# Convolution, sixteen panels' low parts and decay masks: from GpSimd to VectorE in a gated delta rule

## The chip, the cores and the metric

One core of a Trainium2 chip runs the whole model. The metric is the device time of one execution in microseconds; the kernel before took 2576.89 us as the median of three runs (2573.45 to 2579.9). The engines are called PE (TensorE), DVE (VectorE), ACT (ScalarE), POOL (GpSimd) and SP (SyncE, which issues most DMAs).

## What is computed

A two-layer encoder on 1024 tokens of width 1024 in float32: chunked attention, a squared-ReLU MLP, a gated delta rule, a second MLP, with an RMS norm ahead of each. The change is in the delta rule, of which this matters:

```python
qkv = silu(causal_conv(h @ w_in))          # 4 taps: y = sum_j xp[:, j:j+S] * w[j]
q, k, v = split(qkv)                       # 8 heads of 128; q and k are normalised
decay = exp(where(incl, gc[i] - gc[j], -inf))
L = where(strict, (k * beta) @ k.T * decay, 0)      # per chunk of 64
u, w = triangular_solve(I + L, [beta * v, beta * k * exp(gc)])
for chunk:                                 # scan over 16 chunks
    v_new = u - w @ state
    o = (q * exp(gc)) @ state + (q @ k.T * decay) @ v_new
    state = state * g_last + (k * exp(g_last - gc)).T @ v_new
```

The mask of the decay is added before the exponential: 0 where a pair of tokens counts, a large negative number elsewhere.

## The kernel before

**Products.** Float32 products are made of three float32r matmuls: a weight panel of 128 output columns is split into a high part (ACT rounds it, `whi`) and a low part (what is left, `wlo = wraw - whi`, a subtraction of two SBUF tiles), and PE adds high by high, high by low and low by high. A panel has two parts of 128x512. A dense job of the delta rule (one head of k, q, v or z) is two halves of 512 tokens, each 24 matmuls into one of two `acc` banks. The order of jobs is: eight heads of k, then q and v of heads 0 to 2, then z, q, v in turn, and last two panels of the output projection (`dn_ahead`, L1758; the panel's steps are `weights`, L1775, with `low`, L1010).

**Evacuation.** `dn_evac` (L2071) empties a bank. For q, k and v, DVE multiplies the bank with the norm's factor into `xp`, which frees the bank for the half after next; then come the convolution's four taps. Before, ACT makes two of them (`cy`, `cz`), DVE adds one more to each with a scalar_tensor_tensor, and POOL adds the two sums. For k of heads 4 to 7 (`POOLED`, L38) POOL adds twice, ACT makes three taps and DVE one. ACT's silu writes the head.

**Decays.** `dn_loads` (L2012) brings a head's row of cumulated decays into a tile (`row` for even heads, `vT` for odd ones) once the head two before it has its `U`, as the tile is used again. `dn_decays` (L2023) adds the mask in two parts of 128x512, ACT takes exponentials (`row<-row,gcols`), SP stores pieces. `dn_blocks` (L2155) multiplies k by k on PE and DVE multiplies the result with the decays into `U`, of which SP stores the diagonal blocks (`ud`, `u12`), four and two DMAs a head.

**Solves, scans.** `dn_solves` (L2185) waits for the `U` of four heads, loads `fu`, and runs 31 steps of substitution on DVE, a product `ft` and a reduction `fz` each, the last on 128x961. There are two such solves. Behind a solve come the inverses, the preparation of keys, values and queries and, head by head, two at a time, the scans: 16 chunks of PE (`s<-st,WQ`), DVE (`vn`), PE (`s<-vn,kd`), DVE (`st`).

**Order.** One loop (`dn_run`, L1809) emits the dense matmuls and after each lets waiting tasks take a step; a clock with a price for each instruction says which tasks are ready. The engines' programs are fixed by that: each engine takes its instructions in the order in which they were emitted. A change of the engine of an instruction changes the clock and thereby the order of all that follows in the delta rule. The clock has no price for DMAs but fixed sleeps (3.2 us for the row of a head).

Of the kernel before, what the change touches and what calls it, by code (L numbers as in the profile page):

```python
# [10 lines left out]
AF = mybir.ActivationFunctionType  # L11
ALU = mybir.AluOpType
# [8 lines left out]
HB = 512  # L21
# [13 lines left out]
ATT = (3, 2, 0.5, 1, 1, 0.7, 0.6)  # L35
RINGS = {"pt": 2, "po": 2, "sp": 1, "pr": 6, "bias": 3, "thi": 4, "tlo": 3, "oh": 1, "ot": 2}
ENGINES = {"dn_solves": ("vector",), "dn_decays": ("scalar",)}
POOLED = (4, 5, 6, 7)  # L38


def wide(col, p, n):
# [166 lines left out]
class Trunk:  # L208
# [1549 lines left out]
    def dn_ahead(self):  # L1758

        H = 8  # L1760
        self.jobs = jobs = [("k", n) for n in range(H)] + [(c, n) for n in range(3) for c in "qv"]
        for n in range(3, H):
            jobs += [("z", n - 3), ("q", n), ("v", n)]
        jobs += [("z", n) for n in range(5, H)]
        jobs += [("o", m) for m in range(2)]
        raw, panel = {}, {}

        def fetch(n):
            if n < len(jobs):
                c, h = jobs[n]  # L1770
                raw[n] = self.wp.tile([P, KT, P], F32, name=self.nm("wraw"), tag="wraw")
                self.nc.sync.dma_start(
                    raw[n], self.a["w_od"][h] if c == "o" else self.a["w_in"][8 * "qkvz".index(c) + h])

        def weights(n):  # L1775
            hi = self.wp.tile([P, KT, P], F32R, name=self.nm("whi"), tag="whi")
            lo = self.wp.tile([P, KT, P], F32R, name=self.nm("wlo"), tag="wlo")
            panel[n] = hi, lo
            for s in (slice(0, 4), slice(4, 8)):
                self.high(hi[:, s], raw[n][:, s])  # L1780
                yield
                self.low(lo[:, s], raw[n][:, s], hi[:, s], True)
                yield
                yield
            fetch(n + 2)

        def first():

            nc = self.nc
            ab = self.wp.tile([P, KT, P], F32, name=self.nm("wraw"), tag="wraw")  # L1790
            nc.sync.dma_start(ab[:, :, 0:16], self.a["w_ab"])
            for _ in range(8):
                yield
            fetch(0)
            yield
            yield
            self.wab = w = self.wp.tile([P, KT, P], F32R, name=self.nm("whi"), tag="whi")
            nc.gpsimd.memset(w[:, :, 16:32].bitcast(F32), 0.0)
            self.high(w[:, :, 0:16], ab[:, :, 0:16])
            yield  # L1800
            self.low(w[:, :, 32:48], ab[:, :, 0:16], w[:, :, 0:16], True)
            yield
            fetch(1)
            yield from weights(0)

        self.panel, self.weights = panel, weights
        return first()
# [215 lines left out]
    def dn_decays(self, odd):  # L2023

        nc = self.nc
        yield from self.until("rows")
        for h in range(odd, 8, 2):
            yield from self.until("load", h)
            if h < 2:
                yield from self.until("cols")  # L2030
            d = self.heads.pop(("load", h))
            v = d.rearrange("p (q t) -> p q t", t=P)
            for q in range(2):
                u = v[:, 4 * q : 4 * q + 4]
                nc.gpsimd.tensor_tensor(
                    u, u, self.mask.rearrange("p (o t) -> p o t", o=1).broadcast_to([P, 4, P]), ALU.add)
                yield
            for p in range(8):
                nc.scalar.activation(v[:, p], v[:, p], AF.Exp, bias=self.cols[:, 0, h, p : p + 1])
            yield  # L2040
            for e in range(2):
                r = slice(64 * e, 64 * e + 64)
                nc.sync.dma_start(self.decay[h, r], v[r, :, r])
            yield
            self.heads["de", h] = d
            self.mark("de", h)
            yield
# [23 lines left out]
    def dn_evac(self, c, h, half, ps):  # L2071

        nc = self.nc
        s = slice(half * HB, (half + 1) * HB)
        if c == "z":
            if half == 0:
                if h == 1:
                    yield from self.until("solve", 1)
                if h >= 2:
                    yield from self.until("out", h - 2)  # L2080
                self.heads[c, h] = self.dn_out_of(c, h)
            while (c, h) not in self.heads:
                yield
            t = self.heads[c, h][:, s]
            nc.vector.tensor_tensor(t, ps, self.R[:, s], ALU.mult)
            self.give("acc", ps)
            yield
            nc.scalar.activation(t, t, AF.Silu)
        else:
            w = self.convw[:, 8 * "qkv".index(c) + h]  # L2090
            xp = yield from self.take("xp")
            if half == 0:
                nc.vector.memset(xp[:, 0:3], 0.0)
            else:
                nc.vector.tensor_copy(xp[:, 0:3], self.edge[:, HB : HB + 3])
            self.edge = xp
            nc.vector.tensor_tensor(xp[:, 3 : 3 + HB], ps, self.R[:, s], ALU.mult)
            self.give("acc", ps)
            yield
            yt = yield from self.take("cy")  # L2100
            zt = yield from self.take("cz")
            y, z = yt[:, :HB], zt[:, :HB]
            nc.scalar.activation(y, xp[:, 3 : 3 + HB], AF.Copy, scale=w[:, 3:4])
            nc.scalar.activation(z, xp[:, 1 : 1 + HB], AF.Copy, scale=w[:, 1:2])
            yield
            if c == "k" and h in POOLED:
                nc.gpsimd.tensor_tensor(z, y, z, ALU.add)
                yield
                nc.scalar.activation(y, xp[:, 0:HB], AF.Copy, scale=w[:, 0:1])
                nc.vector.scalar_tensor_tensor(z, xp[:, 2 : 2 + HB], w[:, 2:3], z, ALU.mult, ALU.add)  # L2110
            else:
                nc.vector.scalar_tensor_tensor(y, xp[:, 2 : 2 + HB], w[:, 2:3], y, ALU.mult, ALU.add)
                nc.vector.scalar_tensor_tensor(z, xp[:, 0:HB], w[:, 0:1], z, ALU.mult, ALU.add)
            self.give("xp", xp)
            yield
            nc.gpsimd.tensor_tensor(y, y, z, ALU.add)
            self.give("cz", zt)
            yield
            if half == 0:
                for need in self.dn_room(c, h):  # L2120
                    yield from self.until(*need)
                self.heads[c, h] = self.dn_out_of(c, h)
            while (c, h) not in self.heads:
                yield
            nc.scalar.activation(self.heads[c, h][:, s], y, AF.Silu)
            self.give("cy", yt)
            self.silu_at = self.clock.at["scalar"]
        if half == 1:
            self.mark(c, h)
# [532 lines left out]
```

## Time and profile before

The profiled execution took 2579.18 us, its span is 2577.4 us, 2.3 us of the time above the median of the runs. The delta rule with its surroundings runs from about 1210 to 1850 us of the span.

| what | us or share |
|---|---|
| median of the runs (three) | 2576.89 us |
| profiled execution, span | 2579.18 us, 2577.4 us |
| busy share of the span, PE, DVE, ACT, POOL | 96%, 74%, 47%, 50% |
| additions of POOL for the convolution, whole span | 48 of `cy`, 68.9 us, and 8 of `cz`, 11.0 us |
| masks on POOL | 8 on `row`, 10.4 us, and 8 on `vT`, 10.7 us |
| low parts on POOL from 1210 to 1850 us | 66, 89.8 us |

A busy share is an average over stages, and matmuls overlap: PE counts as busy when one is under way. The page's lists of waits name the instruction that came last; the order of an engine's program decides what stands behind it.

### The profile page before, as it was taken

How to read it: one execution, taken by the hardware profiler on the slowest of the kernel's cores; microseconds unless marked ns; L12 is line 12 of the kernel's file. 1: busy time of each engine (PE TensorE's matmuls, PEld its weight loads, DVE VectorE, ACT ScalarE, POOL GpSimd, SP SyncE). 2: the span in 40 equal slices, each digit the busy share in tenths (PEclk: the TensorE clock that was granted, in tenths of full speed). 3: DMA queues.
4: the chain of work that ended last, by engine and by line, in shares of the span. 5: the costliest groups of instructions: out<-in, count | busy, mean ns of one | idle time of the engine just before them, and what ended most of it. 6: DMA issues, size and time to landing. Idle time of an engine off the chain costs nothing.

```text
span 2577.4 us, 36731 instructions
## 1 busy us (share of the span) xinstructions
PE 2472.7 (96%) x12638; PEld 2063.6 (80%) x12638; DVE 1914.8 (74%) x3297; ACT 1210.1 (47%) x2269; POOL 1298.2 (50%) x1090
## 2 busy tenths in 40 slices
PE   8999999999999999998888999999899999999997
PEld 6888888787888788886677788888787888787885
DVE  6665556677878788877578976666678787778877
ACT  6666567535555433334673333333335555433333
POOL 2444355515677476556464333332314766466656
PEclk9999999999999999999998999999999999999998
DMA  4222224424555976743343121122323555967742
GB/s 160 68 65 73 71 84 129 140 82 167 210 203 215 358 233 227 249 147 111 116 142 106 55 82 60 59 85 94 119 98 143 208 209 200 345 235 253 249 160 82
DMA packets 193082, 392.43 MB, mean 152 GB/s; under 512 B 54960, under 2 KB 61552, under 8 KB 192896
## 3 DMA queue, kind: packets, MB, share of 16 engines
q1 hardware_dynamic: 176048, 355.46, 41.0%
q10 hardware_dynamic: 16848, 34.63, 3.4%
q8 instruction: 100, 1.64, 0.3%
q14 instruction: 86, 0.70, 0.1%
HBM read 254.06 MB, written 127.57 MB: 148 GB/s over the span
## 4 chain that ended last, share of the span: by engine, by line
PE 61%; DVE 11%; DMA 3%; issue 3%; ACT 1%; POOL 1%; SPq 0%; ACTq 0%; DVEq 0%; POOLq 0%
PE y L1008 24%; PE z L1008 11%; PE acc L163 9%; PE acc L1008 6%; PE tp L163 4%; PE s L163 3%; DVE ft L163 2%; PE acc L279 1%; PE acc L277 1%; PE acc L278 1%; DVE x L1512 1%; DMA wraw<-in_w_up_dram 1%; DVE wlo L1014 1%; DVE fz L163 1%; DVE xs L393 1%
## 5 line engine op out<-in xcount | busy, mean ns | idle before, releaser
L163 PE MATMUL acc<-xs,whi 128*128 128x512 f32 x1808 | 633.9, 414 | 10.4 <-DVE xp L163 9.8
L163 PEld LDWEIGHTS acc<-xs,whi 128*128 128x128 f32 x1808 | 334.8, 192 | 60.0 <-DVE xp L163 6.1
L163 PE MATMUL acc<-xs,wlo 128*128 128x512 f32 x896 | 369.6, 413 | 2.1 <-POOL wlo L163 2.1
L1008 PE MATMUL y<-xs,whi 128*128 128x512 f32 x1008 | 312.0, 390 | 5.2 <-DVE x L1512 1.8
L163 POOL TENSOR_TENSOR wlo<-wraw,whi 128x512 fp32r<-128x512 f32 x126 | 167.7, 1331 | 246.3 <-ACT whi L163 197.3
L1023 POOL TENSOR_TENSOR s<-wraw 128x256 f32<-128x256 f32 (+1 forms) x93 | 89.4, 962 | 352.9 <-DVE a L1014 171.9
L1014 DVE TENSOR_TENSOR wlo<-wraw,whi 128x512 fp32r<-128x512 f32 (+1 forms) x182 | 209.4, 1151 | 27.3 <-ACT whi L1017 27.3
L1008 PEld LDWEIGHTS y<-xs,whi 128*128 128x128 f32 x1008 | 189.2, 188 | 47.1 <-DVE x L1512 2.6
L1017 ACT ACTIVATE whi<-wraw 128x512 fp32r<-128x512 f32 (+2 forms) x191 | 146.5, 767 | 123.8 <-PE y L1008 86.6
L1008 PE MATMUL y<-xs,wlo 128*128 128x512 f32 x504 | 197.0, 391 | 6.2 <-DVE wlo L1014 6.2
L1008 PE MATMUL y<-xs,a 128*128 128x512 f32 x732 | 189.0, 394 | 10.0 <-DVE x L1512 9.8
L1017 ACT ACTIVATE a<-s 128x256 fp32r<-128x256 f32 x122 | 63.8, 524 | 281.5 <-PE y L1008 141.7
L163 PEld LDWEIGHTS acc<-xs,wlo 128*128 128x128 f32 x896 | 172.6, 193 | 27.0 <-POOL wlo L163 2.5
L1512 DVE TENSOR_TENSOR x<-y,x 128x512 f32<-128x512 f32 x240 | 165.0, 688 | 36.8 <-PE y L1008 28.6
L1008 PEld LDWEIGHTS y<-xs,a 128*128 128x128 f32 x732 | 136.6, 189 | 44.5 <-DVE x L1512 14.2
L1008 PE MATMUL acc<-xs,whi 128*128 128x512 f32 x528 | 162.9, 390 | 0.0
L1008 PE MATMUL y<-xs,ahi 128*128 128x512 f32 x512 | 159.2, 392 | 0.7 <-ACT nt L1201 0.4
L1090 DVE TENSOR_TENSOR c<-c 128x512 fp32r<-128x512 f32 x112 | 132.8, 1203 | 28.5 <-POOL c L1020 28.5
L163 POOL TENSOR_SCALAR pr<-pr,rs 128x640 f32<-128x640 f32 (+4 forms) x128 | 88.1, 692 | 129.4 <-DVE rs L163 96.7
L1008 PE MATMUL z<-xs,whi 128*128 128x512 f32 x480 | 148.8, 391 | 0.0
L163 POOL TENSOR_TENSOR cy<-cy,cz 128x512 f32<-128x512 f32 x48 | 68.9, 1435 | 146.7 <-DVE cz L163 124.3
L163 DVE CUSTOM_DVE_ANT_0 pr<-sp,bias 128x640 f32<-128x640 f32 (+4 forms) x128 | 83.8, 655 | 63.8 <-PE sp L163 62.8
(340 smaller groups left out, 6295.2 us busy)
## 6 DMA issues: line engine op xcount, KB each, us to landing
xs<-gt SPq DMA_DIRECT2D x256, 256.0 KB, 4.9
gt<-c SPq DMA_DIRECT2D x112, 512.0 KB, 3.0
wraw<-in_w_up_dram SPq DMA_DIRECT2D x64, 512.0 KB, 3.5
wraw<-in_w_down_dram SPq DMA_DIRECT2D x64, 512.0 KB, 4.4
r<-gr SPq DMA_DIRECT2D x88, 256.0 KB, 3.4
wraw<-in_w_in_dram SPq DMA_DIRECT2D x32, 512.0 KB, 3.4
gr<-ssum ACTq DMA_DIRECT2D x62, 256.0 KB, 3.2
wraw<-in_w_qkv_dram SPq DMA_DIRECT2D x30, 512.0 KB, 3.4
```

The costliest lines, as they stand in the source:

```text
L163: return call(*args, **more)
L277: nc.tensor.matmul(ps, hi[:, k], xh, start=(k == 0), stop=False)
L278: nc.tensor.matmul(ps, hi[:, k], xl, start=False, stop=False)
L279: nc.tensor.matmul(ps, lo[:, k], xh, start=False, stop=(k == KT - 1))
L393: self.nc.vector.scalar_tensor_tensor(lo, x, w, hi.bitcast(F32), ALU.mult, ALU.subtract)
L1008: nc.tensor.matmul(ps, w[:, k], x, start=bool(first and f), stop=bool(last and e), skip_group_check=True)
L1014: self.nc.vector.tensor_tensor(lo, src, hi.bitcast(F32), ALU.subtract)
L1017: self.nc.scalar.activation(hi, src, AF.Copy)
L1023: self.nc.gpsimd.tensor_tensor(out, x, y, ALU.add)
L1090: nc.vector.tensor_tensor(t[z][:, HB:].bitcast(F32R), t[z][:, HB:], t[z][:, :HB], ALU.subtract)
L1512: nc.vector.tensor_tensor(x, ps, x, ALU.add)
```

## The change

DVE makes what POOL made in three places: the taps of the convolution are one product on ACT and three scalar_tensor_tensor in a chain on DVE (no `cz`, no addition on POOL); the low parts of panels 0 to 15 are subtracted on DVE, later ones stay on POOL; the masks are added on DVE. All else moves only because the clock orders it anew.

```diff
--- before.py
+++ after.py
@@ -35,7 +35,6 @@
 ATT = (3, 2, 0.5, 1, 1, 0.7, 0.6)
 RINGS = {"pt": 2, "po": 2, "sp": 1, "pr": 6, "bias": 3, "thi": 4, "tlo": 3, "oh": 1, "ot": 2}
 ENGINES = {"dn_solves": ("vector",), "dn_decays": ("scalar",)}
-POOLED = (4, 5, 6, 7)
 
 
 def wide(col, p, n):
@@ -1779,7 +1778,7 @@
             for s in (slice(0, 4), slice(4, 8)):
                 self.high(hi[:, s], raw[n][:, s])
                 yield
-                self.low(lo[:, s], raw[n][:, s], hi[:, s], True)
+                self.low(lo[:, s], raw[n][:, s], hi[:, s], n >= 16)
                 yield
                 yield
             fetch(n + 2)
@@ -2032,7 +2031,7 @@
             v = d.rearrange("p (q t) -> p q t", t=P)
             for q in range(2):
                 u = v[:, 4 * q : 4 * q + 4]
-                nc.gpsimd.tensor_tensor(
+                nc.vector.tensor_tensor(
                     u, u, self.mask.rearrange("p (o t) -> p o t", o=1).broadcast_to([P, 4, P]), ALU.add)
                 yield
             for p in range(8):
@@ -2098,23 +2097,12 @@
             self.give("acc", ps)
             yield
             yt = yield from self.take("cy")
-            zt = yield from self.take("cz")
-            y, z = yt[:, :HB], zt[:, :HB]
+            y = yt[:, :HB]
             nc.scalar.activation(y, xp[:, 3 : 3 + HB], AF.Copy, scale=w[:, 3:4])
-            nc.scalar.activation(z, xp[:, 1 : 1 + HB], AF.Copy, scale=w[:, 1:2])
-            yield
-            if c == "k" and h in POOLED:
-                nc.gpsimd.tensor_tensor(z, y, z, ALU.add)
-                yield
-                nc.scalar.activation(y, xp[:, 0:HB], AF.Copy, scale=w[:, 0:1])
-                nc.vector.scalar_tensor_tensor(z, xp[:, 2 : 2 + HB], w[:, 2:3], z, ALU.mult, ALU.add)
-            else:
-                nc.vector.scalar_tensor_tensor(y, xp[:, 2 : 2 + HB], w[:, 2:3], y, ALU.mult, ALU.add)
-                nc.vector.scalar_tensor_tensor(z, xp[:, 0:HB], w[:, 0:1], z, ALU.mult, ALU.add)
+            yield
+            for n in (2, 1, 0):
+                nc.vector.scalar_tensor_tensor(y, xp[:, n : n + HB], w[:, n : n + 1], y, ALU.mult, ALU.add)
             self.give("xp", xp)
-            yield
-            nc.gpsimd.tensor_tensor(y, y, z, ALU.add)
-            self.give("cz", zt)
             yield
             if half == 0:
                 for need in self.dn_room(c, h):
```

Where the masks go. DVE before, from the evacuation `xp` of the seventh half (the first of k of head 3) on; `acc` are PE's banks, `U` the products with decays, `cy` and `cz` the taps:

```order
L163 TENSOR_TENSOR xp_12746<-acc_12675,R_12294 128x512
L163 TENSOR_TENSOR U_12730<-tp_12751,vT_12562 128x512
L163 SCALAR_TENSOR_TENSOR cy_12757<-xp_12746,convw,cy_12757 128x512
L163 SCALAR_TENSOR_TENSOR cz_12758<-xp_12746,convw,cz_12758 128x512
L163 COPY xp_12820<-xp_12746 128x3
L163 TENSOR_TENSOR xp_12820<-acc_12744,R_12294 128x512
L163 TENSOR_TENSOR U_12832<-tp_12833,row_12727 128x512
L163 SCALAR_TENSOR_TENSOR cy_12839<-xp_12820,convw,cy_12839 128x512
L163 SCALAR_TENSOR_TENSOR cz_12840<-xp_12820,convw,cz_12840 128x512
L163 MEMSET xp_12877 128x3
L163 TENSOR_TENSOR xp_12877<-acc_12806,R_12294 128x512
L163 TENSOR_TENSOR U_12832<-tp_12851,row_12727 128x512
```

The masks of these heads stood on POOL, here with what followed them:

```order
L163 TENSOR_TENSOR row_12727<-row_12727,mask 128x512 x2
L163 TENSOR_TENSOR cy_12757<-cy_12757,cz_12758 128x512
L163 TENSOR_TENSOR vT_12777<-vT_12777,mask 128x512 x2
L163 TENSOR_TENSOR wlo_12824<-wraw_12673,whi_12823 128x512
L163 TENSOR_TENSOR cy_12839<-cy_12839,cz_12840 128x512
L163 TENSOR_TENSOR wlo_12824<-wraw_12673,whi_12823 128x512
```

DVE after, from the evacuation of the same half on:

```order
L162 TENSOR_TENSOR xp_12736<-acc_12664,R_12294 128x512
L162 TENSOR_TENSOR row_12708<-row_12708,mask 128x512
L162 TENSOR_TENSOR U_12711<-tp_12739,vT_12569 128x512
L162 SCALAR_TENSOR_TENSOR cy_12745<-xp_12736,convw,cy_12745 128x512 x3
L162 TENSOR_TENSOR row_12708<-row_12708,mask 128x512
L162 COPY xp_12800<-xp_12736 128x3
L162 TENSOR_TENSOR xp_12800<-acc_12734,R_12294 128x512
L162 TENSOR_TENSOR vT_12769<-vT_12769,mask 128x512 x2
L162 SCALAR_TENSOR_TENSOR cy_12811<-xp_12800,convw,cy_12811 128x512 x3
L162 TENSOR_TENSOR wlo_12804<-wraw_12659,whi_12803 128x512
L162 MEMSET xp_12850 128x3
L162 TENSOR_TENSOR xp_12850<-acc_12793,R_12294 128x512
```

The masks of heads 2 (`row`) and 3 (`vT`) now stand between the evacuations, and each convolution is three instructions.

Where the scan of the last head goes. PE before, about the middle of the scan of head 7 (`s` are the banks of the scan, `acc` those of dense products):

```order
L163 MATMUL s_3785_17927<-st_17920,WQ_17613 128x128
L163 MATMUL acc_17844<-xs_11825,whi_17570 128x512
L163 MATMUL acc_17844<-xs_11825,wlo_17571 128x512
L163 MATMUL acc_17935<-xs_17868,whi_17765 128x512 x2
L163 MATMUL s_3790_17942<-vn_12245,kd_17498 128x128
L163 MATMUL s_3785_17927<-vn_12245,qk_12251 128x128
L163 MATMUL acc_17935<-xs_17868,wlo_17766 128x512
L163 MATMUL acc_17935<-xs_17869,whi_17765 128x512 x2
L163 MATMUL s_3792_17954<-st_17946,WQ_17613 128x128
L163 MATMUL acc_17935<-xs_17869,wlo_17766 128x512
```

PE after, at the same stage of the same scan:

```order
L162 MATMUL s_3742_17852<-st_17846,WQ_17582 128x128
L162 MATMUL s_3743_17857<-vn_12245,kd_17465 128x128
L162 MATMUL s_3742_17852<-vn_12245,qk_12251 128x128
L162 MATMUL s_3745_17864<-st_17861,WQ_17582 128x128
L162 MATMUL s_3746_17867<-vn_12244,kd_17465 128x128
L162 MATMUL s_3745_17864<-vn_12244,qk_12251 128x128
L162 MATMUL s_3748_17873<-st_17870,WQ_17582 128x128
L162 MATMUL tp_17876<-ident,o_17263 128x128 x4
L162 MATMUL s_3751_17884<-vn_12245,kd_17465 128x128
L162 MATMUL s_3748_17873<-vn_12245,qk_12251 128x128
```

Between the steps of the scan stood dense matmuls; now there are none, as all 64 halves of q, k, v and z are emitted ahead. Counted in DVE's program, the evacuations (`xp`, `zT`) that stand ahead of a landmark are:

| landmark on DVE | before | after |
|---|---|---|
| last `ft` of the first solve | 22 | 24 |
| first `st` of head 0 | 25 | 29 |
| first `st` of head 1 | 33 | 36 |
| first `st` of head 7 | 61 | 64 |

## Prediction

> **What bounds the kernel now.** I read the page first, then where the landmarks of the delta rule lie, then the busy time between them, then who waits. The landmarks are taken from DVE: the states `st` of the scans (first and last start at the end of the first figures), the first instruction of the first solve, its last long product, and the first `st` of head 1.
>
> ```profile
> L163 DVE SCALAR_TENSOR_TENSOR st<-st,gl,s x112: 330/347/349, 1435.2 to 1838.4; 128x128 f32<-128x128 f32 x112
> L163 DVE COPY st<-s x8: 283/291/292, 1430.8 to 1799.2; 128x128 f32<-128x128 f32 x8
> ```
>
> ```profile
> L163 DVE TENSOR_SCALAR frt<-fu x1: 178/178/178, 1306.4 to 1306.4; 128x32 f32<-128x32 f32 x1
> ```
>
> ```profile
> 1389.81 2.51 DVE L163 TENSOR_TENSOR ft<-fz,fu 128x961 f32<-128x961 f32 x1
> ```
>
> ```profile
> 1505.62 0.29 DVE L163 COPY st<-s 128x128 f32<-128x128 f32 x1 [0.20 <-PE s L163]
> ```
>
> The first solve starts at 1306.4 and its last product at 1389.8; heads 0, 1 and 7 have their first `st` at 1430.8, 1505.6 and 1799.2, and the last `st` of all is at 1838.4. Cut at these points, the busy time of each engine by stretch (length first, then PE, weight loads, DVE, ACT, POOL):
>
> ```profile
> core 0: us, PE busy (x) PEld busy (x) DVE busy (x) ACT busy (x) POOL busy (x), PEclk, DMA share, GB/s
> 1210.00:1306.40 96.40, 86.48 (x398) 71.40 (x398) 50.78 (x103) 57.34 (x104) 49.14 (x42) 0.93 0.41 124
> 1306.40:1389.80 83.40, 70.78 (x320) 58.16 (x318) 80.75 (x133) 45.45 (x80) 46.86 (x33) 0.90 0.35 103
> 1389.80:1430.80 41.00, 34.84 (x290) 29.87 (x291) 33.77 (x76) 16.87 (x29) 20.30 (x18) 0.92 0.37 108
> 1430.80:1505.60 74.80, 69.60 (x480) 56.77 (x478) 70.85 (x131) 25.08 (x49) 26.04 (x19) 1.00 0.18 58
> 1505.60:1799.20 293.60, 286.71 (x1987) 252.46 (x1987) 193.83 (x500) 111.85 (x244) 94.66 (x69) 0.99 0.23 71
> 1799.20:1850.00 50.80, 44.79 (x239) 36.73 (x237) 32.96 (x96) 19.63 (x45) 14.66 (x11) 0.97 0.38 128
> ```
>
> I call the stretches A to F. In E PE is busy 286.7 of 293.6 us: there PE is the bound, and what other engines do costs nothing. In B DVE is busy 80.75 of 83.4 us while PE lacks 12.6: DVE is the bound. In A nobody is full; PE lacks 9.9 us, DVE 45.6. Who holds PE up in A and B, from the list of PE's waits (total, times, longest):
>
> ```profile
> PE acc L163 <- DVE xp L163: 9.8, 2, 5.9
> PE tp L163 <- DVE vb L163: 6.1, 1, 6.1
> ```
>
> What DVE, and below it POOL, waited for in the same time:
>
> ```profile
> DVE cy L163 <- ACT cy L163: 18.0, 5, 10.7
> ...
> DVE U L163 <- DMA u<-U: 7.5, 1, 7.5
> ```
>
> ```profile
> POOL row L163 <- issue: 9.5, 1, 9.5
> POOL row L163 <- DMA row<-grows: 9.3, 2, 6.2
> ```
>
> So A is a chain: a row of decays comes by DMA, POOL masks it, ACT takes its exponential and only then the tap `cy` behind it, DVE waits for `cy` with the next evacuation `xp` behind it, and PE for a bank. A stall of PE costs more than its length; in PE's timeline behind the longest one, and then in a dense stretch:
>
> ```profile
> 1342.49 1.22 PE L163 MATMUL acc<-xs,whi 128*128 128x512 f32 x2 [5.89 <-DVE xp L163]
> 1343.51 0.63 PE L163 MATMUL acc<-xs,wlo 128*128 128x512 f32 x1
> ```
>
> ```profile
> 1328.07 0.62 PE L163 MATMUL acc<-xs,whi 128*128 128x512 f32 x2
> 1328.52 0.39 PE L163 MATMUL acc<-xs,wlo 128*128 128x512 f32 x1
> 1328.75 0.62 PE L163 MATMUL acc<-xs,whi 128*128 128x512 f32 x2
> ```
>
> Behind the stall a matmul lasts 0.63 us instead of 0.39, and the granted clock is 0.90 to 0.93 in A, B and C. In the dense stretch three matmuls take 0.68 us, 0.227 each, so a half of 24 takes 5.45.
>
> **The change part by part.** *Prices.* From the view of the tile `cy` (count, then minimum, median and maximum in ns), the addition on POOL and a tap on DVE:
>
> ```profile
> L163 POOL TENSOR_TENSOR cy<-cy,cz x48: 1258/1287/2792, 1222.8 to 1763.5; 128x512 f32<-128x512 f32 x48
> L163 DVE SCALAR_TENSOR_TENSOR cy<-xp,convw,cy x40: 734/748/1710, 1221.3 to 1761.0; 128x512 f32<-128x512 f32 x40
> ```
>
> and the subtraction of a high part on DVE:
>
> ```profile
> L163 DVE TENSOR_TENSOR xs<-cy,xs x2: 677/685/693, 1826.0 to 1844.5; 128x512 fp32r<-128x512 f32 x2
> ```
>
> Instructions on DVE overlap a little; this one starts 0.60 us before the next, and lasts 0.68:
>
> ```profile
> 1263.54 0.68 DVE L163 TENSOR_TENSOR U<-tp,row 128x512 f32<-128x512 f32 x1
> 1264.14 0.68 DVE L163 TENSOR_TENSOR U<-tp,vT 128x512 f32<-128x512 f32 x1
> ```
>
> So a tap of 0.748 costs DVE about 0.67 us and a low part of 0.685 about 0.61. No mask has run on DVE; it has the size of the low part and two SBUF inputs like it, so 0.61 is taken, between 0.6 and the 1.71 of the slowest tap.
>
> *What POOL does to DVE.* In the solve two products of nearly equal size follow each other, and POOL had started a mask between them:
>
> ```profile
> 1328.03 0.27 DVE L163 TENSOR_TENSOR ft<-fz,fu 128x64 f32<-128x64 f32 x1
> ...
> 1328.58 1.17 DVE L163 TENSOR_TENSOR ft<-fz,fu 128x81 f32<-128x81 f32 x1
> ```
>
> ```profile
> 1328.30 1.29 POOL L163 TENSOR_TENSOR row<-row,mask 128x512 f32<-128x512 f32 x1 [3.23 <-DVE ft L163]
> ```
>
> 64 elements took 0.27 us, 81 took 1.17 and ended at 1329.75, just behind POOL's mask at 1329.59. So a DVE instruction with two SBUF inputs that meets one of POOL waits for its end, on average half of POOL's 1.29. B has 33 instructions on POOL (x33 above); the front part's masks, low parts and additions are all but two of them, and if each held DVE for 0.65 the 31 cost it 20 us. I take 18, as some meet no such instruction, and 8 at the least. The Trainium skill (SBUF — State Buffer, Who interferes with whom) makes of this an exclusive lock for the whole instruction on a port that both engines read through; by that alone all 20 come back, and the sum would be 2 us lower.
>
> *A: +4 us (-6 to +12).* Counted in DVE's program, 14 more taps (33 against 19), 11 low parts and 12 masks stand ahead of the first solve: 14 x 0.67 + 23 x 0.61 = 23 us, which DVE's idle 45.6 can take. What counts is the chain of rows. Head 0's `U` is complete one step behind 1263.54; SP stores it in six DMAs and then issues the row of head 2, whose mask POOL starts at 1275.79, without having waited longer for anything else:
>
> ```profile
> 1266.02 3.57 SPq L2177 DMA_DIRECT2D ud<-U  x4
> 1269.64 1.28 SPq L2181 DMA_DIRECT2D u<-U  x2
> 1270.96 0.60 SPq L1867 DMA_DIRECT2D row<-grows  x1
> ```
>
> ```profile
> 1275.79 2.52 POOL L163 TENSOR_TENSOR row<-row,mask 128x512 f32<-128x512 f32 x2 [9.50 <-issue]
> ```
>
> That is 11 us from `U` to the row of the head after next, while the planner's clock counts 3.2. It stays; but now DVE stands still for it, and with it the evacuation of the eighth half and head 3's `U`, which the front part shows behind masks. Walked through with these prices, DVE waits for a row four times, 4 to 6 us each, within its idle 45.6. The two parts of a mask take 1.2 us instead of 2.5, which shortens each link of the chain by 1.3; but head 3's second `U` stands behind head 4's first mask, which waits for head 2's stores and row, some 5 us. The balance is +4.
>
> *B: +6 us (-2 to +14).* 18 more taps (33 against 15), 12 low parts, 4 masks, two evacuations, two `vb`: 18 x 0.67 + 20 x 0.61 = 24 us. 80.75 + 24 - 18, and 3 us of waiting for the rows of heads 6 and 7, are 90 against 83.4.
>
> *C: +6 us (0 to +10).* Evacuations between the two landmarks: five (29 - 24) against three (25 - 22), two halves more, 10.9 us of PE. PE lacked 6.2 of 41.0 us here and can take that much; 1.5 of new waiting is an allowance.
>
> *D: -9 us (-13 to -3).* One half fewer (7 against 8), -5.4. PE lacked 5.2 us, of which DVE's freed port (about half of 19 POOL instructions leave) saves most; a place where the scans stand alone for three steps costs 2.
>
> *E: +1 us (-4 to +6).* 28 halves as before, PE the bound.
>
> *F: -7 us (-9 to +3).* The three halves that stood here are emitted earlier, and the scan of head 7 stands alone for ten steps. 14 steps took 1838.4 - 1799.2 = 39.2 us, 2.8 each, with dense work between. A step with little of it:
>
> ```profile
> 1823.44 0.29 DVE L163 TENSOR_TENSOR vn<-vb,s 64x128 f32<-64x128 f32 x1
> ...
> 1825.31 0.28 DVE L163 TENSOR_TENSOR vn<-vb,s 64x128 f32<-64x128 f32 x1
> ```
>
> 1.87 us; with PE's clock down, 2.1. Ten of 2.1 and four of 2.8 are 32 against 39.
>
> *Ahead of A* two low parts of panel 0 move to DVE, +-1 us at the end of the first layer's matmuls.
>
> Sum: 4 + 6 + 6 - 9 + 1 - 7 = +1 us. The profiled execution took 2579.18 us, so 2580 by its own time; it lies 2.3 above the median of the runs, so I forecast 2578 us. About 0.3% (7.7 us) is what a measurement of this kernel can tell from no change.
>
> **The rivals.** *Slower: masks hold DVE's queue.* A DVE instruction that waits for a row holds `xp`, `cy` and `U` behind it, whoever needs them. If the rows of heads 2 to 7 each cost the chain 3 us more than walked, A becomes +13 and B +15: the sum is +19, 2596 us. For it: POOL waited 9.5 and 9.3 us for rows, and DVE's own 7.5 us for `U` held all behind. Against it: ACT stood in the same rows' way before, and DVE behind it (18.0). It decides from the point at which DVE's idle time in A and B exceeds 60 us (48.3 now). The Trainium skill (TensorE: Matmul & The Clock Gate, the table at its head) speaks for this rival: VectorE takes its queue strictly in order.
>
> *Faster: port and chain give back more.* If the masks' waits fall into time in which DVE has nothing to do, each of four links in A is 1.3 us shorter (-5 instead of +4); with the full 20 us and no waits B is +1, C with less allowance +4, D and F stay, E as forecast: the sum is -15, 2562 us. For it: the stretched products. Against it: DVE's 45.6 idle us in A are no lock.
>
> *That the change does not do what it says* is ruled out by POOL's program: from the making of the mask to the second solve it holds `ua`, `dc`, `WQ` and memsets alone.
>
> **How the numbers follow.** The forecast has a chance of 0.42, and by itself 2570 to 2584; the slower rival 0.31, the faster 0.27. As the two rivals share 0.58 the range reaches to both, 2562 to 2597. The chances of the three outcomes are those of the cases.
>
> **What would show it.** Right: no product of the first solve stretched by a microsecond; its last product at about 1400; head 1's first `st` within 4 us of 1506; ten steps of head 7 at about 2 us; DVE waiting for DMA at the masks. Wrong: the last product before 1390 (then faster) or behind 1412 (then slower), or E off by over 6 us.

## The result and the profile after

The changed kernel takes 2595.83 us as the median of three runs (2593.45 to 2601.36), beside 2577.1 us for the kernel before in the same measurement; the ratio is 1.0075, with an interval of 1.0061 to 1.0089, that is 16 to 23 us slower. (A fourth run took 4396 us at a granted clock of 0.715 and is left out.) The profiled execution took 2595.83 us, its span is 2593.9 us, against 2579.18 and 2577.4 before: 16.5 us more.

The landmarks on DVE first: the first and the last `st`, then the beginning and the last long product of the first solve. The figures behind the colon are the shortest, median and longest in ns, then the first and the last start.

```profile
L162 DVE SCALAR_TENSOR_TENSOR st<-st,gl,s x112: 328/347/350, 1459.3 to 1853.2; 128x128 f32<-128x128 f32 x112
L162 DVE COPY st<-s x8: 283/288/292, 1451.9 to 1815.8; 128x128 f32<-128x128 f32 x8
...
L162 DVE TENSOR_SCALAR frt<-fu x1: 178/178/178, 1306.4 to 1306.4; 128x32 f32<-128x32 f32 x1
```

```profile
1404.53 1.86 DVE L162 TENSOR_TENSOR ft<-fz,fu 128x961 f32<-128x961 f32 x1
...
1517.95 0.29 DVE L162 COPY st<-s 128x128 f32<-128x128 f32 x1 [1.55 <-PE s L162]
```

Cut at these points, the busy time by stretch (length, then PE, weight loads, DVE, ACT, POOL, then the granted clock). The ends are chosen so that the same work lies in them as before: the first begins 0.2 us ahead of the first instruction of the gates on DVE, `rv` (1210.0 before, 1207.4 here), the last ends 16.5 us behind the 1850 of before.

```profile
core 0: us, PE busy (x) PEld busy (x) DVE busy (x) ACT busy (x) POOL busy (x), PEclk, DMA share, GB/s
1207.40:1306.40 99.00, 88.75 (x413) 72.97 (x413) 67.75 (x143) 48.12 (x93) 1.79 (x6) 0.95 0.46 129
1306.40:1404.50 98.10, 82.75 (x380) 68.44 (x379) 91.64 (x177) 34.34 (x65) 6.76 (x7) 0.92 0.33 94
1404.50:1451.90 47.40, 46.87 (x352) 39.33 (x352) 42.17 (x101) 16.82 (x30) 5.26 (x5) 0.94 0.34 99
1451.90:1517.90 66.00, 57.26 (x392) 45.51 (x391) 60.75 (x110) 17.99 (x37) 17.59 (x13) 0.93 0.19 62
1517.90:1815.80 297.90, 290.42 (x1990) 254.86 (x1989) 205.31 (x519) 101.47 (x228) 70.00 (x51) 0.98 0.20 66
1815.80:1866.50 50.70, 43.20 (x181) 33.81 (x181) 31.83 (x94) 15.97 (x40) 10.69 (x9) 0.74 0.34 124
```

| stretch | before | after | difference | forecast |
|---|---|---|---|---|
| A, to the first solve | 96.4 | 99.0 | +2.6 | +4 |
| B, first solve | 83.4 | 98.1 | +14.7 | +6 |
| C, to the first scan | 41.0 | 47.4 | +6.4 | +6 |
| D, scan of head 0 alone | 74.8 | 66.0 | -8.8 | -9 |
| E, to the scan of head 7 | 293.6 | 297.9 | +4.3 | +1 |
| F, scan of head 7 and end | 50.8 | 50.7 | -0.1 | -7 |

C and D are right within half a microsecond and A within 1.4; B is 8.7 us too small, F 6.9, E 3.3. The start of A lies 2.6 us earlier than before. In the other runs it lies between 1208.1 and 1213.4, so that I give it no meaning: stretches are compared by length, whole kernels by their ratio. Each stretch comes from one profiled execution, and the three runs of the kernel before are up to 6 us apart, so a difference of 2 or 3 us in a stretch proves little by itself: the first solve starts at 1306.4 us of the span in both kernels, although A differs by 2.6.

Two things happened as foreseen. POOL is nearly empty in A and B (1.8 and 6.8 us busy, before 49.1 and 46.9), and the products of the solve are no longer stretched; the two that took 0.27 and 1.17 us before, in DVE's timeline after:

```profile
1337.69 0.26 DVE L162 TENSOR_TENSOR ft<-fz,fu 128x64 f32<-128x64 f32 x1
...
1338.89 0.29 DVE L162 TENSOR_TENSOR ft<-fz,fu 128x81 f32<-128x81 f32 x1
```

And DVE waits for rows at the masks, here with the longest wait at the end of the row (all five waits lie in A):

```profile
DVE row L162 <- DMA row<-grows: 14.4, 3, 6.5
DVE vT L162 <- DMA vT<-grows: 7.9, 2, 4.0
```

In DVE's timeline one of them with what stands behind it, and PE's wait for that `xp`:

```profile
1294.30 0.69 DVE L162 TENSOR_TENSOR row<-row,mask 128x512 f32<-128x512 f32 x1 [4.60 <-DMA row<-grows]
1294.91 0.68 DVE L162 TENSOR_TENSOR U<-tp,vT 128x512 f32<-128x512 f32 x1
1295.52 0.68 DVE L162 TENSOR_TENSOR xp<-acc,R 128x512 f32<-128x512 f32 x1
```

```profile
1296.35 0.70 PE L162 MATMUL acc<-xs,whi 128*128 128x512 f32 x2 [2.39 <-DVE xp L162]
```

DVE did nothing for 4.60 us, though head 3's `U` and an evacuation stood ready behind the mask; PE ran out of banks and waited 2.39 us.

### The profile page after: what moved, and what is told of

Its sections match the earlier page's. It is cut to its first block, busy times and chain, and to the rows that moved or that the text cites. A ratio compares the mean times of both kernels' runs of the same rounds, so it can differ in the third digit from the quotient of the medians.

```text
span 2593.9 us, 36600 instructions
## 1 busy us (share of the span) xinstructions
PE 2486.4 (96%) x12638; PEld 2070.4 (80%) x12638; DVE 1947.6 (75%) x3401; ACT 1168.2 (45%) x2207; POOL 1155.2 (45%) x986
## 5 line engine op out<-in xcount | busy, mean ns | idle before, releaser
L162 POOL TENSOR_TENSOR wlo<-wraw,whi 128x512 fp32r<-128x512 f32 x96 | 126.9, 1323 | 336.6 <-ACT whi L162 242.7
L162 ACT ACTIVATE o<-s 64x128 f32<-64x128 f32 x128 | 34.6, 272 | 208.0 <-PE s L162 192.7
```

What stands on the lines that cost most here:

```text
L162: return call(*args, **more)
```

## The experiments

Three theories were open. *Work*: DVE's added work lengthens the first solve. *Queue*: masks that wait for their rows hold what stands behind them. *Order*: the planner's clock, which now counts more work for DVE, emits dense halves earlier, and that costs time whoever does the work.

### Engine and order apart

The planner's clock can be charged for one engine while another does the work. That makes a square of four kernels: the engine of before or of after, in the order of before or of after. The two new corners are near to that, not exact: in the old order DVE makes the additions while ACT keeps its taps, and in the new order DVE makes two taps for every half, also for k of heads 4 to 7, where before it made one.

```python
def charged(engine, name):
    return Engine(engine.clock, name, engine.real) if isinstance(engine, Engine) else engine
```

**dve_old_order**: the kernel before, with masks, low parts of panels 0 to 15 and the convolution's additions on DVE, charged as POOL's.

```diff
-                nc.gpsimd.tensor_tensor(
+                charged(nc.vector, "gpsimd").tensor_tensor(
                     u, u, self.mask.rearrange("p (o t) -> p o t", o=1).broadcast_to([P, 4, P]), ALU.add)
...
-            nc.gpsimd.tensor_tensor(y, y, z, ALU.add)
+            charged(nc.vector, "gpsimd").tensor_tensor(y, y, z, ALU.add)
```

> Masks, the low parts of panels 0 to 15 and the additions of the convolution run on DVE, but the planner's clock is charged as if POOL made them: PE's, ACT's and SP's programs are those of before, instruction by instruction. If DVE's work in the first solve is the cause (after: 98.1 us from the first frt to the last ft against 83.4), the solve is 8 to 16 us longer than before here too, and the time is 8 to 18 us above before. If the new order is the cause (dense halves emitted earlier, the scan of head 7 left bare), the time is within 5 us of before. If masks that wait for their rows hold DVE's queue, DVE waits for DMA at the masks for more than the 25 us that it waited after, and the front part or the solve is over 15 us longer.

Measured: 1.0038 (1.0026 to 1.0050), about 10 us. A is 100.6 us, B 90.2:

```profile
1209.90:1310.50 100.60, 88.06 (x413) 72.30 (x413) 63.51 (x139) 59.57 (x108) 2.36 (x7) 0.95 0.44 123
1310.50:1400.70 90.20, 69.50 (x305) 55.40 (x304) 81.60 (x163) 43.30 (x77) 7.46 (x6) 0.90 0.32 95
```

B is 6.8 us longer than before, A 4.2. So the engine alone costs half of what the change costs. In B DVE is hardly busier than before (81.60 us against 80.75), as POOL no longer stretches its products, so the added work explains little of it. The 6.8 us are below the 8 to 16 that this theory had, and DVE sits idle at masks there for 6.2 us (2.0 put down to the transfer of a row, 4.2 to nothing that the profile shows).

**pool_new_order**: the changed kernel, with POOL doing the work again (and ACT the second tap), charged as DVE's.

```diff
             nc.scalar.activation(y, xp[:, 3 : 3 + HB], AF.Copy, scale=w[:, 3:4])
+            nc.scalar.real.activation(z, xp[:, 1 : 1 + HB], AF.Copy, scale=w[:, 1:2])
             yield
-            for n in (2, 1, 0):
-                nc.vector.scalar_tensor_tensor(y, xp[:, n : n + HB], w[:, n : n + 1], y, ALU.mult, ALU.add)
+            nc.vector.scalar_tensor_tensor(y, xp[:, 2 : 2 + HB], w[:, 2:3], y, ALU.mult, ALU.add)
+            nc.vector.scalar_tensor_tensor(z, xp[:, 0:HB], w[:, 0:1], z, ALU.mult, ALU.add)
+            self.clock.spend("vector", "scalar_tensor_tensor", (y,), {})
+            nc.gpsimd.real.tensor_tensor(y, y, z, ALU.add)
```

> The counterpart: POOL makes the masks, the low parts and the last addition of the convolution (ACT makes two taps and DVE two, as before), but the clock is charged as in the changed kernel: PE's program is that of the changed kernel, instruction by instruction. If DVE's work is the cause, the time is within 5 us of before. If the order is the cause, it is 12 to 20 us above before, with a last part (first st of head 7 to the end) as long as after, 50.7 us. A mixture would show in the two together: their differences from before should add up to the 19 us of the change, and what they lack or exceed is what order and engine do to each other.

Measured: 1.0046 (1.0034 to 1.0058), about 12 us, a mixture. The two together make 0.84%, the change 0.75% (0.61 to 0.89): they add up within the intervals. All of it in stretches, A to F:

```profile
1213.00:1305.60 92.60, 85.23 (x402) 70.48 (x403) 51.60 (x106) 53.50 (x103) 45.53 (x39) 0.96 0.47 123
1305.60:1402.80 97.20, 83.07 (x391) 69.17 (x389) 87.81 (x149) 41.96 (x77) 53.44 (x35) 0.93 0.40 115
1402.80:1450.60 47.80, 46.11 (x352) 38.78 (x353) 42.16 (x90) 20.12 (x35) 20.85 (x18) 0.96 0.31 88
1450.60:1516.30 65.70, 57.29 (x394) 45.86 (x392) 60.34 (x109) 19.22 (x39) 20.37 (x15) 0.92 0.20 62
1516.30:1814.00 297.70, 288.27 (x1989) 253.29 (x1988) 198.31 (x501) 112.06 (x246) 92.34 (x69) 0.99 0.21 66
1814.00:1862.20 48.20, 39.48 (x184) 30.72 (x182) 31.64 (x94) 15.96 (x40) 10.48 (x9) 0.86 0.37 128
```

B is 97.2 us long, as after (98.1), although POOL works 53 us in it and DVE makes no mask, none of the early low parts and two taps for each half instead of three. What is common to both is the order: PE is busy for 83 us in B, 70.8 before, and there and in C stand the four more evacuations of the table of landmarks (29 ahead of the first `st`, 25 before). Four halves of 5.45 us are 21.8 us; B and C together are 145.0 us against 124.4, 20.6 more. Behind the first `st` four halves fewer are left, and the time from there to the end is 411.6 us against 419.2: only 7.6 of the 21.8 come back (4.6 in the changed kernel, 414.6). That the lengths match is no proof that PE's matmuls make B long: PE is idle for 14 us of it. DVE is the fuller engine, busy for 87.81 us where it was 80.75 (its program has 12 evacuations there instead of 10, with their taps, and `qk` and `vb` of the preparation of heads), and idle for 9.4 us where it was 2.65. `front_hold2` below takes the four halves out of B and C again, and they become only 7.6 us shorter.

### Which of the three parts the engine's half is

Each part alone on DVE, in the order of before, with the same edits as above.

> Before's order (PE's, ACT's programs of before), the masks alone on DVE. By DVE's work: 16 masks of 0.69 us against 16 of 1.29 on POOL that held DVE's products: -2 to +2 us of before. If masks that wait for rows hold DVE's queue: most of the 10 us that all three parts cost in this order, +6 us or more.

> Before's order, the low parts of panels 0 to 15 alone on DVE. By DVE's work: 12 low parts of 0.61 to 0.78 us in the first solve (8.5 us) against about 7 us of POOL's hold on DVE's products: 0 to +5 us of before. If masks are the cause: within 2 us.

> Before's order, the additions of the convolution alone on DVE (two taps on ACT and two on DVE stay, DVE makes the addition too). By DVE's work: 15 additions of 0.69 us in the first solve (10 us) against about 8 us of POOL's hold, so +2 to +8 us of before, the largest of the three, and the three together give the 10 us of all three in this order. If masks are the cause: within 2 us.

| on DVE, order of before | ratio | A | B |
|---|---|---|---|
| masks | 1.0030 (1.0018 to 1.0041) | 98.0 | 88.4 |
| low parts | 0.9991 (0.9983 to 1.0000) | 95.0 | 81.6 |
| additions | 1.0023 (1.0014 to 1.0031) | 98.1 | 83.7 |
| all three | 1.0038 (1.0026 to 1.0050) | 100.6 | 90.2 |

The masks, the smallest work of the three, cost 8 us, as the queue theory had it, and no less than the additions (6 us; the intervals overlap, so which of the two costs more is not shown). Of the three they alone lengthen B, by 5.0 us. Low parts, by the work theory 0 to 5 us dearer, are free or a little better; the additions lie within what the work theory had for them, but B keeps its length with them (83.7 us against 83.4). DVE's waits in A and B with the masks alone on it:

```profile
DVE row L163 <- DMA row<-grows: 21.7, 3, 8.5
DVE vT L163 <- DMA vT<-grows: 11.1, 4, 4.8
DVE row L163 <- issue: 5.6, 1, 5.6
```

38 us of waiting at masks (for 5.6 of them the profile names no transfer), in which nothing behind the mask could start. And in the new order, **mask_pool_new_order**, the changed kernel with the masks alone taken back:

```diff
-                nc.vector.tensor_tensor(
+                charged(nc.gpsimd, "vector").tensor_tensor(
                     u, u, self.mask.rearrange("p (o t) -> p o t", o=1).broadcast_to([P, 4, P]), ALU.add)
```

> The changed kernel with the masks back on POOL, the clock charged as if DVE made them: PE's and ACT's programs are those of the changed kernel. If masks that wait for rows in DVE's queue are the part of the cost that is the engine's (in before's order the masks alone cost 0.30%), the time falls by 5 to 8 us, to 1.0045 to 1.0055 of before, as with all three parts on POOL in this order (1.0046). If it is the work of taps and low parts in the first solve, it stays within 2.5 us of the changed kernel (1.0075).

Measured: 1.0038 (1.0024 to 1.0052), 0.37% under the changed kernel: half of the change's cost goes with 16 instructions. A is 91.8 us instead of 99.0, with the same program on PE; B gains nothing:

```profile
1209.90:1301.70 91.80, 84.86 (x410) 70.46 (x410) 63.17 (x131) 47.30 (x92) 17.82 (x17) 0.98 0.48 133
1301.70:1401.40 99.70, 82.76 (x384) 67.85 (x383) 93.72 (x172) 35.10 (x66) 14.73 (x12) 0.94 0.34 99
```

With the masks back, what remains (1.0038) is not more than the order alone (1.0046). In this order low parts and taps on DVE cost nothing that can be measured.

### One part alone, order left to the planner

> The kernel before with the masks alone on DVE; the planner orders anew. If masks hold DVE's queue they carry most of the change: 10 us or more above before, with DVE waiting for DMA at the masks for over 20 us. If DVE's added work is the cause, 16 masks of 0.69 us are 11 us of work in all, 8 of them around the first solve: within 5 us of before.

> The kernel before with the convolution alone on DVE; the planner orders anew. If DVE's work in the first solve is the cause, the 18 taps more of 0.74 us there (13 us) against half of the 18 us that POOL's additions and low parts cost DVE's products make the solve 3 to 7 us longer, and the time is 3 to 9 us above before. If masks are the cause, within 3 us of before.

Measured: masks alone 1.0099 (1.0086 to 1.0112), the convolution alone 1.0083 (1.0071 to 1.0096), 21 us, outside both of the expectations for it. Each by itself costs as much as the whole change or more (1.0061 to 1.0089; the intervals overlap). For the masks that looks like strong evidence, and isn't: in the order of before the same masks cost 0.30% and the additions 0.23%, so some 0.6 to 0.7% of each is order. In both kernels 24 evacuations stand ahead of the last `ft` (22 before), and 29 and 28 ahead of the first `st` (25). One part is enough to tip the planner, and parts tested that way do not add up.

### Where in the order the time is lost

**after_hold**: the last two dense halves kept for the scan of head 7.

```diff
             for half in range(2):
+                if (c, h) == ("z", 7):
+                    while ("scan", 6) not in self.done:
+                        self.idle()
                 ps = self.dense_bank()
```

> The changed kernel with one edit of the order: the two halves of the last dense panel (z of head 7) are held back until the scan of head 6 is emitted, so that the scan of head 7 has dense matmuls between most of its steps again, as before. If the bare scan with its lower granted clock is where the time goes at the end (in the last part PE lost 24 us against its pace in the rest of the kernel, before 11), the time falls by 5 to 12 us against the changed kernel, to 1.003 to 1.0055 of before. If only DVE's work in the first solve counts, it stays within 3 us of the changed kernel, at 1.0065 to 1.0085.

Measured: 1.0073 (1.0061 to 1.0086), no change. E and F:

```profile
1524.10:1818.60 294.50, 281.60 (x1946) 247.47 (x1945) 201.18 (x517) 99.47 (x225) 68.34 (x49) 0.98 0.21 65
1818.60:1872.30 53.70, 45.62 (x232) 35.57 (x231) 35.33 (x95) 18.46 (x43) 13.76 (x10) 0.97 0.40 141
```

The edit did what it should in F: the granted clock is 0.97 instead of 0.74. But E, which lost two halves (10.9 us of matmuls), became only 3.4 us shorter, and F 3.0 longer. With 26 halves left in E it seems to be the scans that set its length, not the matmuls: PE is busy 281.60 us of 294.5. My expectation for the order theory fails here: the bare tail as such is not where the time is to be had.

**front_hold2**: the evacuations in B and C as before, by two holds in the changed kernel.

```diff
+                if (c, h, half) == ("v", 1, 0):
+                    while ("solve", 0) not in self.done:
+                        self.idle()
+                if (c, h, half) == ("q", 2, 1):
+                    while ("values", 0) not in self.done:
+                        self.idle()
                 ps = self.dense_bank()
```

> The changed kernel with two holds in the order: the first half of v of head 1 waits for the first solve, the second half of q of head 2 for the values of head 0, so that 22 evacuations stand ahead of the last ft and 25 ahead of the first st of head 0, as before (24 and 29 in the changed kernel). From the first st of head 0 to the last st of all the runs so far took 399 to 410 us, whatever dense work was left for it. If that stage has its own length and dense halves ahead of it only delay it, the first st of head 0 comes 6 to 14 us earlier against the start than in the changed kernel and the time falls by 5 to 12 us, to 1.003 to 1.0055 of before. If PE is the bound there, as I forecast, what the front part loses in matmuls is added behind it: the same time as the changed kernel or up to 8 us more.

Measured: 1.0126 (1.0112 to 1.0140), 13 us above the changed kernel. B to E:

```profile
1310.90:1405.50 94.60, 70.67 (x332) 59.67 (x331) 88.60 (x172) 33.57 (x63) 5.87 (x7) 0.86 0.35 98
1405.50:1448.80 43.30, 33.36 (x273) 27.27 (x273) 32.86 (x74) 10.84 (x19) 6.61 (x6) 0.88 0.30 84
1448.80:1525.90 77.10, 72.04 (x484) 58.74 (x482) 72.38 (x139) 22.49 (x45) 13.24 (x10) 1.00 0.15 47
1525.90:1833.80 307.90, 296.07 (x2037) 259.06 (x2035) 219.96 (x521) 106.29 (x237) 77.83 (x56) 1.00 0.22 69
```

The first `st` comes 7.6 us earlier against the end of A than in the changed kernel (137.9 us instead of 145.5), as the theory of a stage with its own length said, and then the time from there to the end is 435.3 us instead of 414.6: the stage has no length of its own, and the kernel is even slower than the other theory had it (up to 8 us). The four halves moved from B and C to D and E (9 and 30 halves against 7 and 28), which became 11.1 and 10.0 us longer: 21.1 us for 21.8 us of matmuls, where B and C had given back 7.6. So behind the first `st` these halves are paid in full, and in B and C at about a third. In B PE is busy for 70.67 us, as before, and B is still 94.6 us long, with DVE busy for 88.60. The two halves and the 12 us of PE with them were not what made B long; that kernel's F is bare too and 50.3 us long.

**front_hold2_mask_pool** has the holds and the masks on POOL.

> Both edits of the two runs beside this one. If they act on different things, their gains add up: 10 to 18 us below the changed kernel, 1.0005 to 1.0035 of before. If both only shorten the same first solve, no more than the larger of the two alone.

Measured: 1.0109 (1.0094 to 1.0125), not below the changed kernel, since the hold was no gain; beside front_hold2 the masks' return takes A from 99.4 us to 92.3, as it did above, though the whole kernels' intervals overlap.

**after_warm**: is it the granted clock that slows the bare steps?

```diff
+                    if h == 7:
+                        for _ in range(3):
+                            nc.tensor.real.matmul(ps, self.ident, self.ident, start=True, stop=True)
                     nc.tensor.matmul(ps, wq, st, start=True, stop=False, skip_group_check=True)
...
+                    if h == 7:
+                        for _ in range(3):
+                            nc.tensor.real.matmul(s2, self.ident, self.ident, start=True, stop=True)
                     nc.tensor.matmul(s2, kd[:, p], vn, start=True, stop=True)
```

> The changed kernel with 90 more matmuls, all in the scan of head 7: three of 128x128 by the identity, whose product nobody reads, into the bank of the scan ahead of s<-st,WQ and ahead of s<-vn,kd, where PE waits for DVE (0.3 us for st, 0.37 us for vn, in the changed kernel). Everything else, and the order, is the changed kernel's. If the lower granted clock makes the bare steps slow (2.47 us in the middle of the scan, 1.85 us at its start), ten of them come back to 1.9 to 2.1 us, the last part is 4 to 6 us shorter, and the time is 1.005 to 1.0065 of before. If the steps are as long as DVE and PE need in turn whatever the clock, the fillers only stand in the way: the last part is 0 to 4 us longer, 1.0075 to 1.009.

Measured: 1.0075 (1.0062 to 1.0089), the same as the changed kernel. PE's timeline in the bare scan of the changed kernel:

```profile
1823.88 0.46 PE L162 MATMUL s<-st,WQ 128*128 128x128 f32 x2 [0.31 <-ACT o L162]
...
1825.73 0.46 PE L162 MATMUL s<-st,WQ 128*128 128x128 f32 x2 [0.31 <-ACT o L162]
1826.57 0.80 PE L162 MATMUL s<-vn,kd 128*128 128x128 f32 x2 [0.38 <-DVE vn L162]
...
1827.90 0.77 PE L162 MATMUL s<-st,WQ 128*128 128x128 f32 x2
...
1830.37 0.77 PE L162 MATMUL s<-st,WQ 128*128 128x128 f32 x2
```

and with the fillers:

```profile
1829.12 0.83 PE L2444 MATMUL s<-ident 128*128 128x128 f32 x6
1829.79 0.39 PE L162 MATMUL s<-st,WQ 128*128 128x128 f32 x2
...
1831.13 0.83 PE L2444 MATMUL s<-ident 128*128 128x128 f32 x6
```

The theory of the clock is right and the remedy of no use. In the changed kernel a step takes 1.85 us (1823.88 to 1825.73) until the clock falls at 1826.5 (the granted clock is 0.50 from there to 1850.4), then 2.47 (1827.90 to 1830.37), as the same matmuls last 0.77 to 0.80 us instead of 0.46. With the fillers they last 0.39 in this stretch and a step takes 2.01 (1829.12 to 1831.13), but six fillers are 1.3 us of it, twice the 0.7 us of waiting that they were to fill. The granted clock is 0.98 in F, and yet the 14 steps take 37.3 us, as without fillers (37.4); F is 49.9 us instead of 50.7. Fewer fillers were not tried.

## Why the prediction was right or wrong, step by step

I forecast 2578 us and no change; it is slower by 0.75%. The range of 2562 to 2597 holds the median of 2595.83, but only just, by the end that the slower rival had set (2596 us, chance 0.31). That its figure is met is luck: it had +13 for A and +15 for B, 9 us of each by masks, and E and F as in the forecast. A is +2.6; B is +14.7 but no shorter with the masks on POOL; E and F are 3 and 7 us above the forecast. Of the signs that I had named, DVE waits at the masks and the last product came at 1404.5, nearer to 1400 than to 1412; but head 1's first `st` came 12 us behind 1506, and bare steps took 2.47 us.

- **A, +4: right in kind (+2.6).** Head 3's second `U` was to stand about 5 us behind head 4's first mask, and DVE waited 4.60 us there. I had four waits of 4 to 6 us; there are five, of 3.3 to 6.5. But I set the waits against shorter links of the chain; with the masks on POOL the same program on PE has an A of 91.8 us. So the masks cost 7.2 us in it, and the rest of the change gives 4.6 back: the small balance is that of two terms larger than mine.
- **B, +6: the step that failed.** I wrote B as DVE's work, "80.75 + 24 - 18, and 3 us of waiting". The engine was right, the terms were not. The sum leaves out the 2.65 us in which DVE was idle there before (83.4 - 80.75); with them it is 92.4. DVE's work grew by 10.9 us (80.75 to 91.64), not by 6: the relief from POOL is there, as in the products of the solve, before and after,

```profile
L163 DVE TENSOR_TENSOR ft<-fz,fu 128x1 f32<-128x1 f32 (+29 forms) x30 | 30.0, 1001 | 0.4
L162 DVE TENSOR_TENSOR ft<-fz,fu 128x1 f32<-128x1 f32 (+29 forms) x30 | 22.1, 738 | 0.2
```

  but twelve low parts took 9.3 us, not 7.3, and four `qk`, which the new order brings into B, were not in my count:

```profile
L162 DVE TENSOR_TENSOR wlo<-wraw,whi 128x512 fp32r<-128x512 f32 x12 | 9.3, 779 | 0.0
L162 DVE TENSOR_TENSOR qk<-tp,dc 64x256 f32<-64x256 f32 x4 | 1.7, 416 | 0.0
```

  The taps were dear too: three in a chain take 2.23 us, from this row to the start of the next, not three times 0.67, which is 2.4 us more for the eleven halves:

```profile
1349.15 2.32 DVE L162 SCALAR_TENSOR_TENSOR cy<-xp,convw,cy 128x512 f32<-128x512 f32 x3
1351.38 0.70 DVE L162 TENSOR_TENSOR ft<-fz,fu 128x289 f32<-128x289 f32 x1
```

  And DVE's idle time grew by 3.8 us, to 6.46, but not for the rows of heads 6 and 7: it waits for no row in B, and 3.5 us of it are put down to PE. 83.4 + 10.9 + 3.8 are the 98.1. That B is 90.2 us in the order of before, as I forecast, is luck: there DVE is busy for 81.60 us only and waits 6.2 at masks.
- **C, +6: right**, by counting halves against PE: two more, and PE is busy for 46.87 us of 47.4. **D, -9: right in the number, not for the reason given.** I had 5.4 us for one half and most of the rest from DVE's freed port. PE's busy time fell by 12.3 us (69.60 to 57.26), and what it lacks grew from 5.2 to 8.7 us; with POOL at work (20.37 us of the stretch) D is 65.7 us, just as short. That the terms met is luck.
- **E, +1: 3 us too little.** "PE the bound" holds upwards: two halves more cost 10.0 us, two fewer gain 3.4. The count of halves alone does not set E: with the masks alone on DVE and the order left to the planner it has 26 and takes 302.0 us.
- **F, -7: the other step that failed.** "Ten of 2.1 and four of 2.8 are 32 against 39": the ten steps took 24.7 us and the four 12.7, together 37.4 (first `st` at 1815.8, last at 1853.2), since a bare step is 2.47 us once the granted clock has fallen (0.74 in F, 0.97 before), and from the last `st` to the end it takes 13.3 us instead of 11.6. The Trainium skill (TensorE: Matmul & The Clock Gate, What's actually happening) says that a monitor lowers the clock when PE has not been busy lately; the trace agrees, and after_warm shows it by the counter-test. But the deeper fault is that the three halves which left F had cost nothing there: F is 50.8 us with three, 53.7 with two and 50.7 with none. I credited 7 us for taking away what was free.
- **The slower rival** named the right mechanism for half of the cost: masks in DVE's queue, 0.30% by themselves in the old order and 0.37% in the new. Its price and its place were off (it had 9 us more than the forecast in A and 9 in B; in the changed kernel the masks cost 7 us of A and nothing in B), and so was its point of decision: DVE's idle time in A and B is 38 us (31.25 and 6.46), not over 60, yet the waits cost. Idle time that DVE spends anyway and time in which it holds `xp` back are not the same thing. That VectorE takes its queue strictly in order, which the Trainium skill says (TensorE: Matmul & The Clock Gate, the table at its head), is what the 4.60 us above show.
- **The faster rival**: POOL's hold on DVE's products is gone, but of the three parts only the low parts came out below the kernel before, by 0.09%, with an interval that touches 1.

What stays open: the order costs 0.46% as a sum, and B is 13.8 us longer by it with POOL at work; in DVE's terms that is 7.1 us of work and 6.7 of idle time, and no run takes these apart. It is not by the four halves in B and C alone: taking them out there made the kernel 13 us slower. A kernel with the front of before, the dense tail of before and DVE's taps was not run. The best of all kernels is the one before with the low parts of panels 0 to 15 on DVE in the old order, 0.9991, and its interval touches 1.

## What to carry to other kernels

Where a planner sets the order, an edit is two edits; charge its clock for the old engine while the new one works, and the reverse, and each half can be measured. Price a piece of work that moves by what it costs where it arrives, and credit nothing where it left a place in which something else took that long anyway: four halves taken out of B and C gave back 7.6 us and cost 21.1 in D and E. Think twice before an instruction that waits for a transfer goes on an engine whose queue feeds the bound, however short it is: here 16 masks of 0.69 us cost 8 to 10 us.

## What the runs showed of the hardware

- A scan in which PE waits for DVE some 0.7 us of every 1.85 keeps the high clock for a few steps only (bare from about 1821, slower from 1826.5, when the granted clock falls to 0.50) and then runs its matmuls at 0.77 to 0.80 us a pair instead of 0.46; fillers that nobody reads keep it up (granted clock 0.98 in F).
- Chained taps on DVE, each of which reads what the one ahead wrote, do not overlap: 0.78 us from start to start at a length of 0.75. The last of the three, which the next instruction does not read, gives way after 0.67 (it starts at 1350.72, the next at 1351.38), and independent instructions of 0.68 start 0.60 apart.
